# HGRN outputs summed from the last chunk, and weight splits and row-tile steps held behind the next operand at stage boundaries

## The chip, the cores and the metric

The kernel runs on one core of one Trainium2 chip. The metric is device time in microseconds (us) of one execution. Five engines work side by side, each through its own queue in order: TensorE (PE, matmuls; PEld is its weight load), VectorE (DVE), ScalarE (ACT), GpSimd (POOL) and SyncE (SP, which here issues all the DMAs). A matmul writes into one of 8 PSUM banks; everything else lies in SBUF.

## The reference, cut to what matters

A backbone of two layers over 512 latent tokens and 256 context tokens of width 1024. Each layer is a half-step SwiGLU, a token mixer and a half-step SwiGLU; each of these ends in a post-norm update. The mixer of layer 0 is a bidirectional HGRN (a gated linear recurrence in both directions, 8 heads), that of layer 1 a chunked spatial-gating MLP.

```python
def modulate(x, m, k):
    return x * (1 + m[..., 3 * k + 1, :]) + m[..., 3 * k, :]

def post_norm_update(x, y, m, k, g, b):
    return layer_norm(DN_ALPHA * x + m[..., 3 * k + 2, :] * y, g, b)

def macaron_half_ffn(x, m, k, w_in, w_out, g, b):
    return post_norm_update(x, 0.5 * swiglu(modulate(x, m, k), w_in, w_out), m, k, g, b)

# HGRN, per head: S_t = diag(f_t) S_{t-1} + k_t v_t^T,  o_t = S_t^T q_t, in chunks
o = (o_intra + o_inter)                 # inside a chunk + from the state before it
o = o_forward + reversed(o_backward)    # both directions
o = o * rsqrt(mean(o * o) + eps) * norm_w * silu(g)
```

For a token chunk s of a head the output is thus a sum of three products: the forward queries with the forward state before s, the backward queries with the backward state after s, and the scores inside the chunk with the values.

## The kernel before

**Precision.** Every big matmul is done in three: each operand is split into a high part (`fp32r`, rounded) and the rest. `split` (L134) makes the high part on ACT (L135) and the rest on DVE (L136). `mm3` (L146) multiplies high by high (L148), high by rest (L149) and rest by high (L150). `unit` (L139) loads one weight block of 128x1024 into a tile `raw` (a ring of 3) by an SP DMA (L141), takes a tile `w` (a ring of 6) and splits the one into the other.

**A stage's end.** `OutPhase.run` (L406) multiplies the hidden rows `h` by the output weights into four PSUM banks `y` (one for each 128-token tile), one half of the width (`hf`) after the other. Of the second half, the last `tail` pairs of blocks are not multiplied as they come: `held` (L426) loads and splits them first, and then goes tile by tile, so that the first token tiles are finished early. Then come, in the order in which the code is written:

- `operand_cols` (L430) and `nxt.load()` (L431): the next stage's first weights are loaded and split;
- `part` for each tile; where the next stage has `hold` set, the last two held blocks of the last tile are kept back as `rest` (L434);
- `done(0)` (L439): `evac` (L353) and `norm` (L364) of tiles 0 and 1: L357, L359 or L361, and L362 on DVE for each half tile, L367 and L369 on DVE, a power on POOL (L371), and L381 on DVE, which writes the normalised rows;
- the next operand: `operand` (L383), eight steps of two 128-column blocks for two token tiles. One step is four transposes on PE (L391), one scaling on DVE (L403) and one on ACT (L401), and a split (L135, L136). With `hold`, two of these steps come first, then `rest`, then `done(1)` (tiles 2 and 3), then the six other steps mixed with `nxt.staged`, the next stage's first matmuls, in the order that the string `order` gives (L508, L827).

The next stages: `FeedContext` (L779) and `HgrnValues` (L796) have `hold = False`; `FeedSums` (L741) and `GateIn` (L824) have it set. The `OutPhase` behind the HGRN has `tail=4` (L1306) and a `FeedSums` behind it; the two of the first SwiGLU have `tail=2` (L1045 for the latent tokens, with `FeedContext` next, and L1054 for the context, with `HgrnValues` next: its weights are `hg_wi`); the others with a next stage have `tail=3`. The very last has `tail=4` and no next stage. `FeedSums.rest` goes on with `seven` (L655), whose first call queues its DVE work behind the latest split.

**The HGRN.** The loop over heads (L1309) works on the projections of head h while head h-1 is finished. `latent_states` (L1252) goes through the four token chunks, forward for direction 0 and backward for direction 1; at each chunk it writes the scaled state `Sc` (L1262), which `outputs` (L1273) multiplies. So the forward states come in the order of chunks 0, 1, 2, 3, and the backward ones 3, 2, 1, 0. `outputs` sums the three products of each chunk into a bank `po` (L1280 forward, L1281 backward, L1282 inside the chunk) for s = 0 to 3, and normalises them (L1285 ACT, L1287 and L1288 DVE, L1290 POOL, L1292 DVE). `gated` (L1296), a head later, transposes the result (`pto`, L1298).

**What sets the order.** The code above is traced in program order; a scheduler then fixes each engine's queue, taking of the instructions that it holds to be ready the one traced first. On the chip the queues are fixed. `tc.issue_after(ins)` puts what is traced inside its block on the engine of `ins` behind `ins` in that engine's queue: it orders, and adds no wait for the end of `ins`. Other engines, the DMA queue among them, are not bound by it.

## Time and profile before

| | us |
|---|---|
| median of 3 runs | 2452.76 |
| lowest and highest of them | 2450.28, 2453.76 |
| the profiled execution, its own time | 2451.28 |
| its span, first to last instruction | 2449.6 |
| PE busy | 2415.6 (99%) |
| DVE busy | 1963.5 (80%) |
| ACT busy | 1151.4 (47%) |

The profiled execution's time lies 1.5 us below the median. Matmuls overlap in the records: one of 512 columns is shown with some 0.39 us, while in a full pipeline the next starts 0.227 us later, so a gap on PE is read from the starts. The view of waits shows what an engine was idle for, the chain of waits which work set the end, and the view by windows the busy time of each engine and the granted TensorE clock (PEclk) in one stretch.

The stretches that the change touches, by the span's clock: the end of the first SwiGLU for the latent tokens at 365 to 390 us, its end for the context at 550 to 585, the HGRN loop at 640 to 955, and the boundary behind it at 955 to 1030.

### The profile page before, as it was taken

To read this page: it belongs to the slowest core of one execution; us is meant where nothing else is said; L and a number is where in the kernel's file an instruction comes from. 1 tells how busy PE (TensorE), PEld (TensorE's weight loads), DVE (VectorE), ACT (ScalarE), POOL (GpSimd) and SP (SyncE) were. 2 spreads that over 40 slices of the span, in tenths; PEclk is the share of its full clock that TensorE was granted. 3 is DMA by queue.
4 is the path that set the end of the run, shared out by engine and by line. 5 is a ranking of instruction groups with operands and counts; after the bars stand their busy time and mean duration, and the time that the engine had idled before them with its cause. 6 is when DMAs were issued, how large, how long until landed. Compare 5 with 4: busy or idle time off the path is not lost.

```text
span 2449.6 us, 38155 instructions
## 1 busy us (share of the span) xinstructions
PE 2415.6 (99%) x14907; PEld 2185.6 (89%) x14907; DVE 1963.5 (80%) x3532; ACT 1151.4 (47%) x1784; POOL 34.0 (1%) x57
## 2 busy tenths in 40 slices
PE   7999999999999999999999999999999999999998
PEld 5888889987888888999988999988999988999987
DVE  7965679686488886988796988898898777988785
ACT  4222334454454452555643655544654443555641
POOL 0000000000000000000000000000000000000000
PEclk9999999999999999999999999999999999999999
DMA  8866465874211113433474333584323365333452
GB/s 324 299 204 202 164 196 191 285 243 149 70 54 57 61 52 112 152 111 104 139 237 154 108 104 104 156 261 140 122 84 96 116 219 173 132 118 104 138 162 79
DMA packets 107429, 366.01 MB, mean 149 GB/s; under 512 B 12472, under 2 KB 13808, under 8 KB 107248
## 3 DMA queue, kind: packets, MB, share of 16 engines
q1 hardware_dynamic: 107248, 363.58, 45.0%
q8 instruction: 116, 1.90, 0.3%
q14 instruction: 65, 0.53, 0.1%
HBM read 350.92 MB, written 12.61 MB: 148 GB/s over the span
## 4 chain that ended last, share of the span: by engine, by line
PE 83%; DVE 11%; ACT 3%; issue 2%; DMA 1%; POOL 0%; SPq 0%; DVEq 0%; POOLq 0%; ACTq 0%
PE y L150 9%; PE y L148 9%; PE y L149 9%; PE psf L150 6%; PE psf L149 6%; PE psf L148 5%; PE psc L148 5%; PE psc L149 5%; PE psc L150 5%; PE pse L150 3%; PE pse L148 3%; PE pse L149 3%; DVE w L136 1%; PE psa L150 1%; PE psa L149 1%
## 5 line engine op out<-in xcount | busy, mean ns | idle before, releaser
L136 DVE TENSOR_TENSOR w<-raw,w 128x1024 fp32r<-128x1024 f32 (+3 forms) x447 | 502.2, 1128 | 156.4 <-ACT w L135 152.3
L135 ACT ACTIVATE w<-raw 128x1024 fp32r<-128x1024 f32 (+3 forms) x447 | 436.4, 978 | 384.0 <-PE y L150 77.7
L150 PE MATMUL y<-w,hs 128*128 128x512 f32 x984 | 383.5, 390 | 1.2 <-DVE hs L136 1.1
L148 PE MATMUL y<-w,hs 128*128 128x512 f32 x984 | 383.9, 390 | 0.6 <-ACT hs L135 0.6
L149 PE MATMUL y<-w,hs 128*128 128x512 f32 x984 | 382.9, 389 | 0.0
L150 PEld LDWEIGHTS y<-w,hs 128*128 128x128 f32 x984 | 184.6, 188 | 42.0 <-DVE hs L136 3.8
L135 ACT ACTIVATE hs<-h 128x512 fp32r<-128x512 f32 (+1 forms) x220 | 126.4, 587 | 202.4 <-PE y L150 181.7
L148 PEld LDWEIGHTS y<-w,hs 128*128 128x128 f32 x984 | 184.7, 188 | 39.3 <-ACT hs L135 0.9
L149 PEld LDWEIGHTS y<-w,hs 128*128 128x128 f32 x984 | 184.8, 188 | 38.0
L148 PE MATMUL psf<-xm,w 128*128 128x512 f32 (+1 forms) x544 | 191.7, 356 | 14.3 <-ACT xm L1009 10.9
L150 PE MATMUL psf<-xm,w 128*128 128x512 f32 (+1 forms) x544 | 192.1, 354 | 1.2 <-DVE w L136 1.2
L149 PE MATMUL psf<-xm,w 128*128 128x512 f32 (+1 forms) x544 | 192.2, 354 | 0.1
L136 DVE TENSOR_TENSOR hs<-h,hs 128x512 fp32r<-128x512 f32 (+1 forms) x220 | 135.6, 637 | 65.7 <-ACT hs L135 65.5
L148 PE MATMUL psc<-f,w 128*128 128x256 f32 x544 | 154.3, 284 | 0.5 <-ACT sc L716 0.5
L150 PE MATMUL pse<-f,w 128*128 128x256 f32 x544 | 154.2, 284 | 0.1
L148 PE MATMUL pse<-f,w 128*128 128x256 f32 x544 | 154.0, 283 | 0.0
L150 PE MATMUL psc<-f,w 128*128 128x256 f32 x544 | 153.9, 283 | 0.0
L149 PE MATMUL psc<-f,w 128*128 128x256 f32 x544 | 153.9, 283 | 0.0
L149 PE MATMUL pse<-f,w 128*128 128x256 f32 x544 | 153.9, 283 | 0.0
L148 PE MATMUL psc<-xm,w 128*128 128x256 f32 x532 | 151.6, 285 | 0.6 <-ACT sc L716 0.6
L150 PE MATMUL psc<-xm,w 128*128 128x256 f32 x532 | 150.5, 283 | 0.0
L149 PE MATMUL psc<-xm,w 128*128 128x256 f32 x532 | 150.5, 283 | 0.0
(342 smaller groups left out, 6020.1 us busy)
## 6 DMA issues: line engine op xcount, KB each, us to landing
raw<-in_ffn_w_in SPq DMA_DIRECT2D x159, 512.0 KB, 4.6
raw<-in_ffn_w_out SPq DMA_DIRECT2D x110, 512.0 KB, 4.1
mraw<-in_mod_w SPq DMA_DIRECT2D x80, 512.0 KB, 4.6
rawu<-in_mod_w SPq DMA_DIRECT2D x64, 512.0 KB, 3.9
rawu<-in_ffn_w_in SPq DMA_DIRECT2D x60, 512.0 KB, 3.6
x<-x SPq DMA_DIRECT2D x36, 512.0 KB, 4.4
raw<-in_hg_wf SPq DMA_DIRECT2D x32, 512.0 KB, 3.5
raw<-in_cm_w_out SPq DMA_DIRECT2D x24, 512.0 KB, 4.7
```

Source lines behind the costliest of these rows:

```text
L135: nc.scalar.activation(dst_hi, src, AF.Copy)
L136: latest[0] = nc.vector.tensor_tensor(dst_lo, src, dst_hi.bitcast(F32), ALU.subtract)
L148: nc.tensor.matmul(ps, ah, bh, start=start, stop=False, **kw)
L149: nc.tensor.matmul(ps, ah, bl, start=False, stop=False, **kw)
L150: return nc.tensor.matmul(ps, al, bh, start=False, stop=stop, **kw)
```

## The change

1. In `outputs` the four chunks are summed in the order 3, 2, 1, 0.
2. Where the next stage is not on `hold` (the two ends of the first SwiGLU), all that `nxt.load()` traces on DVE is queued behind the latest split's DVE half, and all that it traces on ACT behind that split's ACT half. The latest split there is the last one of the held operands.
3. At the boundary behind the HGRN (`tail=4` and a next stage) only two of the four weight blocks are loaded at the old place. The DVE work of the first two operand steps and of `done(1)` (tiles 2 and 3) is queued behind the normalisation of tile 1, and the other two weight blocks are loaded after `done(1)`, their DVE halves queued behind the first operand step's split.

At the boundaries with `tail=3` the code does what it did.

```diff
     def split(dst_hi, dst_lo, src):
-        nc.scalar.activation(dst_hi, src, AF.Copy)
+        latest_hi[0] = nc.scalar.activation(dst_hi, src, AF.Copy)
         latest[0] = nc.vector.tensor_tensor(dst_lo, src, dst_hi.bitcast(F32), ALU.subtract)
...
-            nc.vector.tensor_scalar(z, z, mv[:, 0:1], rstd, ALU.subtract, ALU.mult)
+            self.normal = nc.vector.tensor_scalar(z, z, mv[:, 0:1], rstd, ALU.subtract, ALU.mult)
...
                 self.cols = operand_cols(self.l, self.j, *self.after, self.cond)
-                nxt.load()
+                if self.tail > 3:
+
+                    nxt.load(2)
+                elif nxt.hold:
+                    nxt.load()
+                else:
+                    with tc.issue_after(latest[0].ins), tc.issue_after(latest_hi[0].ins):
+                        nxt.load()
...
-                for i in range(2):
-                    self.operand(*steps[i])
-                for r in rest:
-                    self.part(*r)
-                close()
-                nxt.enter()
-                done(1)
+                with tc.issue_after(self.normal.ins) if self.tail > 3 else ExitStack():
+                    los = [self.operand(*steps[i]) for i in range(2)]
+                    for r in rest:
+                        self.part(*r)
+                    close()
+                    nxt.enter()
+                    done(1)
+                if self.tail > 3:
+                    with tc.issue_after(los[0].ins):
+                        nxt.load(2)
...
                 po = bank("po")
-                for s in range(NT):
+
+                for s in reversed(range(NT)):
                     o = po[:, s * P : (s + 1) * P]
```

## The prediction

> **What bounds the kernel now.** First the page: engine totals and the chain that ended last.

> ```profile
> PE 2415.6 (99%) x14907; PEld 2185.6 (89%) x14907; DVE 1963.5 (80%) x3532; ACT 1151.4 (47%) x1784; POOL 34.0 (1%) x57
> PE 83%; DVE 11%; ACT 3%; issue 2%; DMA 1%; POOL 0%; SPq 0%; DVEq 0%; POOLq 0%; ACTq 0%
> ```

> PE is the bound, and the change removes no matmul. It can only win places where PE stands still, so I next read PE's waits.

> ```profile
> ...
> PE pt L391 <- DVE x L381: 3.7, 4, 3.0
> PE po L1281 <- DVE Sc L1262: 2.5, 7, 0.4
> PE y L150 <- DVE hs L136: 1.1, 2, 0.6
> PE y L148 <- ACT hs L135: 0.6, 1, 0.6
> ```

> The row left out at the top is the kernel's start, which stays. These four are the change's three places. This view counts from a matmul's modelled end; below I use the starts, which show more.

> **Part 1, the context's end (L431, tail 2).** The chain of waits, then PE and ACT in order of time:

> ```profile
> 560.33 4.84 DMA raw<-in_hg_wi
> ...
> 565.19 1.07 ACT w L135
> ...
> 566.28 0.65 DVE w L136
> ...
> 567.42 0.43 DVE hs L136
> ```

> ```profile
> 565.49 0.50 PE L150 MATMUL y<-w,hs 128*128 128x512 f32 x1
> 566.60 0.50 PE L148 MATMUL y<-w,hs 128*128 128x512 f32 x1 [0.61 <-ACT hs L135]
> 566.94 0.39 PE L149 MATMUL y<-w,hs 128*128 128x512 f32 x1
> 567.90 0.50 PE L150 MATMUL y<-w,hs 128*128 128x512 f32 x1 [0.57 <-DVE hs L136]
> ...
> 571.47 0.39 PE L150 MATMUL y<-w,hs 128*128 128x512 f32 x1
> 571.70 0.39 PE L148 MATMUL psv<-w,xm 128*128 128x512 f32 x1
> ```

> The last operand's split waits on ACT and then on DVE behind the split of an `hg_wi` block that only the next stage needs. Full pace is 0.227 us (571.47 to 571.70). PE loses 566.60 - 565.49 - 0.227 = 0.88 and 567.90 - 566.94 - 0.227 = 0.73, together 1.61 us. The new edges put the four `hg_wi` splits behind that operand on both engines, so both losses go. What is late next: the four splits themselves. The blocks have three `raw` tiles, so the fourth block's DMA waits for the first block's split. That now ends about 567.4 (my estimate: the operand done near 565.3, when its own 0.8 on DVE no longer waits, then 1.07 on ACT and about 1.1 on DVE); with 4.84 for the DMA, 1.07 and 1.2 for its two halves it is ready at 574.5. `psv` would start at 571.70 - 1.61 = 570.1 and reach its fourth block after 18 matmuls, at 574.2. So 0.3 us may come back; bounds 0 (PE does the second tile's products first) and 1.61 (all comes back). I take a **gain of 1.4**. This stage's `evac` has three of these splits ahead of it, as traced first; its rows are not transposed before 582.58 (row in part 2), 10.9 after `y` ends: nothing.

> The same edit at 365 to 390 us holds two weight splits (1.2 us of DVE each) back until the last operand, just ahead of the evacuations. It costs nothing as long as this slack lasts:

> ```profile
> 379.07 0.81 DVE L381 TENSOR_SCALAR x<-x,mv,rstd 128x1024 f32<-128x1024 f32 x1
> 384.58 1.91 PE L391 MATMUL pt<-ident,x 128*128 128x128 f32 x16
> ```

> Tile 1's rows are done at 379.9 and transposed from 384.6: 4.7 us of cover, filled by the context's matmuls. Two splits in front would take 2.4 of it. With the cover gone it would cost up to 1.2.

> **Part 2, the boundary behind the HGRN.** The chain here (DVE's first row is a weight split, cut short by the chain's next step), and then the same stretch by windows (us; busy us of PE, PEld, DVE, ACT, POOL; PEclk; DMA):

> ```profile
> 979.81 0.28 DVE w L136
> ...
> 980.95 0.81 DVE x L381
> 981.76 1.13 DVE w L136
> 982.89 0.60 DVE st L362
> 983.50 0.59 DVE t L357
> 984.21 0.61 DVE x L359
> 984.88 0.66 DVE st L362
> 985.55 0.82 DVE x L381
> 986.42 1.55 PE pt L391 x6
> ...
> 1003.42 0.69 DVE xm L136
> ...
> 1027.53 0.39 PE pse L150
> ```

> ```profile
> 978.00:1003.40 25.40, 21.66 (x147) 19.43 (x147) 19.80 (x38) 11.76 (x19) 2.52 (x4) 0.93 0.40 145
> 1003.40:1027.50 24.10, 24.04 (x201) 23.83 (x199) 24.10 (x40) 15.29 (x25) 0.00 (x0) 1.00 0.40 141
> ```

> Transposes in order of time, here and at the context's end:

> ```profile
> 986.42 2.82 PE L391 MATMUL pt<-ident,x 128*128 128x128 f32 x12 [3.02 <-DVE x L381]
> 582.58 1.91 PE L391 MATMUL pt<-ident,x 128*128 128x128 f32 x16
> ```

> On the way to tile 1's rows (L381 at 985.55) DVE does two weight splits (1.13 each) and three steps of tile 2 (L357, L359, the second L362: 1.9). The edit takes all of these, some 4.2 us, out of the way: rows ready near 982.2 instead of 986.4. On PE's side the prize is larger. It waits 3.02, and after it the 12 transposes take 2.82 where 16 took 1.91: at a start every 0.11 that is 1.3 us too slow, and the windows show why, a PEclk of 0.93 over the stretch against 1.00. By PE's rows alone 4.3 us could go.

> But the work taken out is not gone: the 4.2 us of DVE move to between tile 1's rows and the last operand step, whose split is the row at 1003.42. From there the chain runs on DVE for 24 us without a hole (24.10 of 24.10 busy), since `seven` queues behind that split, and PE meets it at 1027.53. A faster PE before that only waits there. So the gain of this part is what the split at 1003.42 gains, and DVE has 25.40 - 19.80 = **5.6 us** idle before it. Part of the idle time is round trips (transpose, DVE, ACT, ACT, DVE), which stay. Bounds: a gain of 4.2, if all moved work falls into holes; a loss of 2.4, if the two late splits land in front of tile 3's rows and leave the holes behind. The rows lie in between; filling about half of the 4.2 gives a **gain of 2.1**.

> [...] The trace's slow transposes after 3.02 us of waiting agree with a clock halved there.

> Moved DMAs: the two late blocks' loads are bound by `raw` tiles as before (ready-first on SP), and the two `raw` tiles that they free come back late by as much as the splits move, for weights of the second and third hidden block, whose splits stand behind those at 1003.42 and after: hidden. The token rows' stores, which might now stand behind these loads on SP, are read back only by the next stage's end: nothing, unless they hold SP for 20 us.

> **Part 3, outputs from chunk 3.** In order of time: one head, its last backward state and PE around it; then the first use of head 6's outputs:

> ```profile
> 884.74 0.39 PE L148 MATMUL psfl<-xm,w 128*128 128x512 f32 x1
> ...
> 885.14 0.31 DVE L1262 TENSOR_SCALAR Sc<-S,se 128x128 f32<-128x128 f32 x1
> ...
> 885.50 0.49 PE L1281 MATMUL po<-Sc,B 128*128 128x128 f32 x2 [0.37 <-DVE Sc L1262]
> 885.83 0.39 PE L1282 MATMUL po<-v,ssum 128*128 128x128 f32 x2
> ```

> ```profile
> 928.50 0.39 PE L150 MATMUL y<-w,ht 128*128 128x512 f32 x1
> ...
> 929.15 0.66 PE L1298 MATMUL pto<-ident,on 128*128 128x128 f32 x4 [0.27 <-DVE on L1292]
> ```

> PE stands 885.50 - 884.74 - 0.227 = 0.53 us per head, seven times (the row of waits has 7): 3.7 us. The state waited for is that of chunk 0, the last of the backward direction. Chunk 3 first means that it is needed last, but it is still needed at the same place in DVE's queue, and the three chunks that now run earlier (2 us of PE) push out as much `psfl` filler. The filler stands in the queue up to where the scheduler held the state to be ready, in the middle of an `mm3` (L148, then L1281): PE will again arrive there 0.53 early, with the last chunk. I take **0** for the seven heads, bounds 3.7 (the wait goes) and -0.7 (a second break in each head: the pair at 885.50 takes 0.49 where the next pair takes 0.39, so a break costs 0.1 beside the wait). Three quarters of the sums are then done before the break, so the normalisation starts up to 2 us earlier, and the wait at 929.15 (0.65 - 0.227 = 0.42) goes: a **gain of 0.4**.

> **The sum.** 1.4 + 2.1 + 0.4 = 3.9 us off the profiled execution's 2451.28: 2447.4. That execution lies 1.5 below the median of 2452.76; off the median it is **2448.9**, my forecast, about 2449.

> **Rivals.**
> - *The heads' wait really goes.* For it: chunk 3's states are both there early, and only a quarter of the sums depends on the last one. Against: queues fixed by a schedule that is 0.53 off. Time: 3.7 more, 2445.2.
> - *All of the moved DVE work hides.* For it: 5.6 us of holes. Against: round trips. Gain 1.4 + 4.2 + 0.4 = 6.0: 2446.8.
> - *Nothing at the HGRN's boundary.* PE's wait moves from tile 1's rows to the two late weight splits, and operand 7's split comes no earlier: 2451.0.
> - *The clock halves again.* After tile 1's rows PE has transposes and short waits instead of matmuls; if that stretch counts as idle, 12 slow transposes cost 1.3 again: 2450.2. [...] In this trace 16 transposes at 582.58 ran at full pace, but behind matmuls.
> - *Slower.* The two late splits (2.4) come before tile 3's rows and the second half of the operand steps, whose holes stay: the row at 1003.42 comes 2.4 later, and the DVE chain behind it carries that to PE at 1027.53; with the clock's 1.3 on top the loss is 3.7, against gains of 1.8. It decides once those splits delay 1003.42 by more than 1.8. Time: 2452.76 + 1.9 = 2454.7.

> **Chances.** Forecast 0.40, heads 0.18, all hidden 0.13, nothing at the boundary 0.14, clock 0.06, slower 0.09. A measurement of this kernel can tell about 0.2% (4.9 us) from no change. Faster by more: the heads and all-hidden cases, and 0.12 of the forecast's (its own range is a gain of 2 to 6, 2446.8 to 2450.8): 0.43. Slower by more: 0.04, the slower case were it 3 us worse. Same: 0.53. The range reaches from 0.7 us of run-to-run room below the heads' case to just short of the slower one: 2444.5 to 2454.

> **What would show it.** In the changed kernel's profile: (1) no `hg_wi` split ahead of the context's last `hs` pair, and `y` matmuls 0.227 us apart up to `psv`. (2) L381 of tile 1 within 1 us of 982 on today's clock, no PE wait of 3 us before L391, PEclk 1.00; the last operand step's split some 2 us nearer to the HGRN's end, and still a DVE chain without a hole behind it. (3) L1281's wait still once per head, now at the last chunk; `pto` at the loop's end without a wait. It is wrong if the 0.53 before L1281 falls below 0.2, or if the split at 1003.42 moves by nothing or by 4 us.

## The result: slower, and only in the heads

| | us |
|---|---|
| before, median of 4 runs | 2453.26 |
| changed, median of 4 runs | 2482.91 |
| ratio, 95% interval | 1.0122 [1.0104, 1.0139] |
| span of the profiled execution, before and changed | 2449.6, 2481.5 |

The change costs 29.7 us. The page of the changed kernel, engine totals and the chain that ended last:

```profile
PE 2429.1 (98%) x14907; PEld 2199.3 (89%) x14907; DVE 1962.4 (79%) x3532; ACT 1150.8 (46%) x1784; POOL 34.1 (1%) x57
...
PE 86%; DVE 9%; ACT 3%; issue 1%; DMA 1%; POOL 0%; SPq 0%; DVEq 0%; POOLq 0%; ACTq 0%
```

PE has as many instructions as before and is 13.5 us longer busy with them: they ran slower. Then its waits (us in total, times, the longest):

```profile
PE po L1291 <- DVE Sc L1272: 25.9, 7, 3.7
...
PE pt L391 <- DVE x L381: 0.7, 3, 0.3
```

The lines have moved by ten or eleven: L1291, L1292 and L1293 are now the forward product, the backward one and the one inside the chunk (L1280 to L1282 before), and L1272 writes the scaled state (L1262 before). The wait of 3.0 us before L391 is gone, as forecast, and so are those of `y` for `hs`. The wait before `po` has grown from 0.4 to 3.7 us in each of seven heads (the eighth and last, whose queue holds other work there, waits in neither kernel), and it is another wait: L1291 is the *forward* product. One head, PE in order of time:

```profile
858.98 0.39 PE L150 MATMUL psq<-xm,w 128*128 128x512 f32 x1
863.07 0.80 PE L1291 MATMUL po<-Sc,B 128*128 128x128 f32 x2 [3.70 <-DVE Sc L1272]
863.66 0.63 PE L1292 MATMUL po<-Sc,B 128*128 128x128 f32 x2
...
866.65 0.63 PE L149 MATMUL psq<-xm,w 128*128 128x512 f32 x1
...
869.70 0.40 PE L150 MATMUL psq<-xm,w 128*128 128x512 f32 x1
```

and DVE in the same head:

```profile
860.05 0.28 DVE L1272 TENSOR_SCALAR Sc<-S,se 128x128 f32<-128x128 f32 x1
...
861.64 0.28 DVE L1272 TENSOR_SCALAR Sc<-S,se 128x128 f32<-128x128 f32 x1
...
862.75 0.67 DVE L1272 TENSOR_SCALAR Sc<-S,se 128x128 f32<-128x128 f32 x3
```

`psq` is the bank of two projections, q's and g's, each of 24 matmuls. The `psq` at 858.98 is the last of q's. All 24 matmuls of g's projection stand in the queue behind the first products of `po`. The first product is that of chunk 3 with its forward state, and this is the *last* state of the forward direction: the first of the three at 862.75, done at 863.03, 0.04 before PE starts. PE's queue holds nothing ahead of that product that PE could do until then. When it starts, an `mm3` matmul takes 0.63 instead of 0.39. The view by windows shows why; the rows are steps of 3.413 us, at whose ends the clock changes in this head (us; busy us of PE, PEld, DVE, ACT, POOL; PEclk; DMA share, GB/s):

```profile
854.64:858.05 3.41, 3.41 (x16) 2.82 (x15) 3.41 (x9) 0.06 (x1) 0.00 (x0) 1.00 0.32 130
858.05:861.46 3.41, 1.32 (x6) 0.75 (x4) 3.41 (x12) 2.05 (x5) 0.00 (x0) 1.00 0.00 0
861.46:864.88 3.41, 1.80 (x8) 1.80 (x9) 3.41 (x12) 2.42 (x5) 0.00 (x0) 0.50 0.00 0
864.88:868.29 3.41, 3.41 (x13) 3.00 (x12) 2.77 (x8) 0.00 (x0) 0.00 (x0) 0.50 0.52 154
868.29:871.70 3.41, 3.41 (x21) 2.97 (x20) 0.00 (x0) 0.43 (x1) 0.00 (x0) 1.00 0.00 0
```

After each wait the clock is at half for one or two such steps. All the seven stretches together, the first and the last of them and the sum:

```profile
690.80:697.62 6.83, 6.10 (x22) 5.52 (x23) 5.30 (x15) 1.54 (x3) 0.00 (x0) 0.50 0.28 77
...
946.80:953.62 6.83, 5.13 (x19) 4.75 (x20) 6.26 (x19) 2.50 (x5) 0.00 (x0) 0.50 0.25 77
sum 37.55, PE 31.27 PEld 29.42 DVE 34.00 ACT 11.97 POOL 0.00; mean PE 4.47 PEld 4.20 DVE 4.86 ACT 1.71 POOL 0.00
```

31.27 us of PE's work ran at a PEclk of 0.50; in the head above, matmuls of 512 columns then start 0.43 us apart (867.08 and 867.51) instead of 0.227. Taken as twice the time, from the 0.50 alone, that gives an estimate of 15.6 us for the clock. The waits grew by 25.9 - 2.5 = 23.4. Together 39.0 us for the seven heads; measured, by the stages below, are 37.6.

The stages, by the starts of three instructions: `psv`'s first matmul (the first product of `HgrnValues`), the last head's `pto`, and the first `psc` behind the HGRN (a bank of the SwiGLU that follows). Before:

```profile
954.72 0.28 PE L1298 MATMUL pto<-ident,on 128*128 128x128 f32 x1
...
1015.28 0.28 PE L148 MATMUL psc<-xm,w 128*128 128x256 f32 x1
```

and changed:

```profile
569.53 0.39 PE L148 MATMUL psv<-w,xm 128*128 128x512 f32 x1
...
990.13 0.27 PE L1309 MATMUL pto<-ident,on 128*128 128x128 f32 x1
...
1047.34 0.28 PE L148 MATMUL psc<-xm,w 128*128 128x256 f32 x1
```

`psv` starts 2.2 earlier (571.70 before); the heads take 420.6 instead of 383.0, 37.6 more; from the last `pto` to `psc` it takes 57.2 instead of 60.6, 3.4 less. By these two traces parts 1 and 2 gained what they were meant to and a little more; part 3 lost nearly seven times as much.

### The profile page after: what moved, and what is told of

Read it like the earlier page. It is cut to its first block, busy times and chain, and to the rows that moved or that the text cites. A ratio compares the mean times of both kernels' runs of the same rounds, so it can differ in the third digit from the quotient of the medians.

```text
span 2481.5 us, 38157 instructions
## 1 busy us (share of the span) xinstructions
PE 2429.1 (98%) x14907; PEld 2199.3 (89%) x14907; DVE 1962.4 (79%) x3532; ACT 1150.8 (46%) x1784; POOL 34.1 (1%) x57
## 4 chain that ended last, share of the span: by engine, by line
PE 86%; DVE 9%; ACT 3%; issue 1%; DMA 1%; POOL 0%; SPq 0%; DVEq 0%; POOLq 0%; ACTq 0%
PE y L150 9%; PE y L148 9%; PE y L149 9%; PE psf L150 5%; PE psf L148 5%; PE psf L149 5%; PE psc L148 5%; PE psc L150 5%; PE psc L149 5%; PE pse L150 2%; PE pse L148 2%; PE pse L149 2%; PE psa L150 1%; PE psa L149 1%; PE psa L148 1%
## 5 line engine op out<-in xcount | busy, mean ns | idle before, releaser
L136 DVE TENSOR_TENSOR w<-raw,w 128x1024 fp32r<-128x1024 f32 (+3 forms) x447 | 500.5, 1124 | 162.0 <-ACT w L135 161.2
L135 ACT ACTIVATE w<-raw 128x1024 fp32r<-128x1024 f32 (+3 forms) x447 | 436.0, 978 | 389.6 <-DMA raw<-in_ffn_w_in 80.3
L148 PE MATMUL y<-w,hs 128*128 128x512 f32 x984 | 383.7, 390 | 0.0
L150 PE MATMUL y<-w,hs 128*128 128x512 f32 x984 | 383.2, 390 | 0.0
L149 PE MATMUL y<-w,hs 128*128 128x512 f32 x984 | 382.9, 389 | 0.0
L135 ACT ACTIVATE hs<-h 128x512 fp32r<-128x512 f32 (+1 forms) x220 | 126.6, 588 | 211.1 <-PE y L150 192.7
L150 PEld LDWEIGHTS y<-w,hs 128*128 128x128 f32 x984 | 184.6, 188 | 39.7 <-DVE hs L136 1.3
L148 PEld LDWEIGHTS y<-w,hs 128*128 128x128 f32 x984 | 184.8, 188 | 38.4
L149 PEld LDWEIGHTS y<-w,hs 128*128 128x128 f32 x984 | 184.8, 188 | 37.8
L148 PE MATMUL psf<-xm,w 128*128 128x512 f32 (+1 forms) x544 | 191.5, 357 | 14.3 <-ACT xm L1019 10.8
L150 PE MATMUL psf<-xm,w 128*128 128x512 f32 (+1 forms) x544 | 192.6, 355 | 0.8 <-DVE w L136 0.7
L149 PE MATMUL psf<-xm,w 128*128 128x512 f32 (+1 forms) x544 | 192.3, 355 | 0.4 <-DVE xm L136 0.4
L136 DVE TENSOR_TENSOR hs<-h,hs 128x512 fp32r<-128x512 f32 (+1 forms) x220 | 135.2, 633 | 71.0 <-ACT hs L135 70.7
L148 PE MATMUL psc<-f,w 128*128 128x256 f32 x544 | 154.5, 284 | 0.7 <-ACT sc L726 0.7
L150 PE MATMUL pse<-f,w 128*128 128x256 f32 x544 | 154.3, 284 | 0.2 <-DVE w L136 0.2
L148 PE MATMUL pse<-f,w 128*128 128x256 f32 x544 | 154.0, 283 | 0.0
L150 PE MATMUL psc<-f,w 128*128 128x256 f32 x544 | 153.9, 283 | 0.0
L149 PE MATMUL psc<-f,w 128*128 128x256 f32 x544 | 153.9, 283 | 0.0
L149 PE MATMUL pse<-f,w 128*128 128x256 f32 x544 | 153.9, 283 | 0.0
L148 PE MATMUL psc<-xm,w 128*128 128x256 f32 x532 | 151.6, 285 | 0.6 <-ACT sc L726 0.6
L150 PE MATMUL psc<-xm,w 128*128 128x256 f32 x532 | 150.5, 283 | 0.0
L149 PE MATMUL psc<-xm,w 128*128 128x256 f32 x532 | 150.5, 283 | 0.0
```

The source lines that it names most:

```text
L135: latest_hi[0] = nc.scalar.activation(dst_hi, src, AF.Copy)
L136: latest[0] = nc.vector.tensor_tensor(dst_lo, src, dst_hi.bitcast(F32), ALU.subtract)
L148: nc.tensor.matmul(ps, ah, bh, start=start, stop=False, **kw)
L149: nc.tensor.matmul(ps, ah, bl, start=False, stop=False, **kw)
L150: return nc.tensor.matmul(ps, al, bh, start=False, stop=stop, **kw)
```

## The experiments

The same starts for every kernel that follows, in us; the first column runs from the last `pg` ahead of `psv` (a short matmul in the context's end, at 536.25 before) to `psv`, and each row is one profiled execution:

| kernel | `pg` to `psv` | heads | last `pto` to `psc` |
|---|---|---|---|
| before | 35.4 | 383.0 | 60.6 |
| changed | 33.4 | 420.6 | 57.2 |
| parts 1 and 2 alone | 34.6 | 382.9 | 57.4 |
| reversed order alone | 36.8 | 420.0 | 60.5 |
| bank opened | 33.3 | 384.2 | 57.3 |
| one step of g first | 33.2 | 384.0 | 57.7 |
| order 1, 2, 3, 0 | 33.5 | 387.1 | 57.4 |
| old order, in the next head | 32.9 | 378.9 | 57.1 |
| reversed, in the next head | 33.4 | 378.4 | 57.5 |
| 3 matmuls of g ahead | 33.4 | 414.9 | 57.2 |
| 6 matmuls of g ahead | 34.4 | 406.1 | 57.4 |
| 12 matmuls of g ahead | 32.9 | 387.0 | 57.5 |

### Which part costs

Parts 1 and 2 alone:

```diff
-                for s in reversed(range(NT)):
+                for s in range(NT):
                     o = po[:, s * P : (s + 1) * P]
```

> The changed kernel with the chunks summed in the old order 0, 1, 2, 3: parts 1 and 2 alone. Theory A (the reversed order alone made the loss; parts 1 and 2 gained 2.1 us up to psv and some 2.5 us behind the HGRN, by the starts in the two traces): 2453.3 - 4.6 = 2448.7, between 2447.5 and 2450; the seven waits before po are back at 0.4 each, 2.5 us in total, PEclk 1.00 through the head loop. Rival B (the edits of parts 1 and 2 changed the queues inside the head loop): waits of 3 us and a time above 2470 stay.

2446.74 us against 2451.54 for the kernel before, ratio 0.9978 [0.9969, 0.9988]. PE's wait before `po` is the old one, for the backward state (L1292):

```profile
PE po L1292 <- DVE Sc L1272: 2.4, 7, 0.4
```

The reversed order alone, in the kernel before:

```diff
-                for s in range(NT):
+                for s in reversed(range(NT)):
                     o = po[:, s * P : (s + 1) * P]
```

> The kernel before with the chunks summed in the order 3, 2, 1, 0 and nothing else. Theory A (the seven heads cost 37.6 us more by the starts of pto in the two traces, whatever the rest does): 2453.3 + 37.6 = 2490.9, between 2488 and 2493. Rival B (it costs this much only together with parts 1 and 2): under 2475.

2487.9 us, ratio 1.0145 [1.0132, 1.0158], with the same wait as in the changed kernel:

```profile
PE po L1280 <- DVE Sc L1262: 25.9, 7, 3.7
```

Both times lie just below their ranges (2447.5 to 2450, and 2488 to 2493). The kernel before ran at 2451.54 beside these, 1.7 under the 2453.3 from which the expectations were worked out, so the differences count: 4.8 gained where 4.6 was expected, 36.4 lost where 37.6 was. Theory A holds both times. Part 3 costs 36.4 us by itself, parts 1 and 2 gain 4.8. The parts add up: 36.4 - 4.8 = 31.6 against the 29.7 of the whole, within the intervals of some 0.2%.

### Why g's projection stood behind the products

All PSUM tiles of this kernel share one ring of eight banks. `outputs` is traced ahead of g's projection. Theory C: a bank is given to the tile traced later only once the earlier one has its own, and `po` takes its bank with its first instruction. In the old order that is the forward product of chunk 0, whose state is there early; the trace of before shows it as a single pair (one product is two matmuls) between q's last `psq` and g's first:

```profile
876.76 0.39 PE L150 MATMUL psq<-xm,w 128*128 128x512 f32 x1
876.99 0.38 PE L1280 MATMUL po<-Sc,B 128*128 128x128 f32 x2
877.13 0.48 PE L148 MATMUL psq<-xm,w 128*128 128x512 f32 x1
```

Reversed, the first instruction needs the last forward state, and g's matmuls would wait with it. The rival D is that the schedule merely took that state to be ready 3.7 us too early. Two edits tell them apart. The first gives `po` its bank early, by an instruction that needs nothing:

```diff
                 po = bank("po")
+                nc.tensor.transpose(po[:, 3 * P :], ident, ident)
```

> The changed kernel, order 3, 2, 1, 0, with one more 128x128 transpose of the identity into the bank po ahead of the products (overwritten by them). Theory C (the banks of one ring are given out in the order traced, so g's projection, traced behind po, can't be queued before po's first instruction, and that now needs the forward direction's last state): with the bank opened 14 of g's 24 matmuls (3.2 us) are queued ahead of the first product; its wait falls from 3.7 to about 0.5 to 0.7 per head, the clock stays at 1.00, and the time comes to that of parts 1 and 2 alone plus 7 x (0.1 for the transpose and 0 to 0.6 of wait): 2449.5 to 2453.5. Rival D (the schedule simply holds that state to be ready 3.7 us too early): a wait of over 3 us stays behind g's matmuls and the time is above 2470.

2447.24 us, ratio 0.9983 [0.9974, 0.9991]: below the expected 2449.5 to 2453.5, also by 0.2 when the range is counted from the 2446.74 of parts 1 and 2 alone. The transpose stands where the forward product of chunk 0 stood, 14 of g's matmuls follow, and then the products in the reversed order. PE in order of time and its waits:

```profile
837.78 0.27 PE L1288 MATMUL po<-ident 128*128 128x128 f32 x1
841.65 0.49 PE L1291 MATMUL po<-Sc,B 128*128 128x128 f32 x2 [0.38 <-DVE Sc L1272]
```

```profile
PE po L1291 <- DVE Sc L1272: 2.6, 7, 0.4
```

The second edit adds no instruction. The first of g's eight `mm3` is traced ahead of `outputs`; the bank tile is still asked for where it was:

```diff
-                    on = outputs(h - 1, prev)
-                    g, last = proj_silu(h - 1, 3, "g")
+                    ons, po = [], bank("po")
+                    g, last = proj_silu(h - 1, 3, "g", 1, lambda: ons.append(outputs(h - 1, prev, po)))
+                    on = ons[0]
...
         for k in range(KD):
             last = feat_k(ps, w, xm, k, c0, c1)
+            if k + 1 == at:
+                then()
```

> The changed kernel, order 3, 2, 1, 0, with only the tracing order turned: the first 3 of g's 24 matmuls are traced ahead of the outputs, and nothing is held. Theory C (g's projection is held back only because its bank is given out behind po's): g's bank is then given out first, 14 of its matmuls stand ahead of the first product, the wait of 3.7 us falls to 0.4 to 0.7 per head and the clock stays full: the time of the kernel with the opened bank less 7 x 0.1 for its transposes, 2446.5, between 2445 and 2449. Rival M (it was the added transpose that helped, by another way): waits of over 3 us and over 2470.

2447.68 us, ratio 0.9985 [0.9976, 0.9995]:

```profile
PE po L1292 <- DVE Sc L1274: 3.7, 7, 0.6
```

Rivals D and M fall: with the bank taken early the schedule itself puts 14 matmuls, 3.2 us, ahead of the first product, so it had the state's time to within 0.4 to 0.6 us. What it did not do, with the bank not yet taken, was put g's matmuls there. That the order in which banks are given out is the reason is what all three kernels of this part agree with; no run shows the inside of the scheduler. The expectation for the second kernel was 2446.5 and it came out 1.2 above, inside its range.

A third order tests theory C where nobody meant to help. Chunk 1 opens the bank:

```diff
-                for s in reversed(range(NT)):
+                for s in (1, 2, 3, 0):
```

> The changed kernel with the chunks summed in the order 1, 2, 3, 0. Theory C: the bank is opened by the forward state of chunk 1, which by the changed kernel's trace is there 1.1 us after q's projection ends (860.33 against 859.21): a wait of 1.1 for it, then 25 matmuls, and some 0.5 before the backward state of chunk 0: 7 x (1.6 - 0.4) over parts 1 and 2 alone, 2446.7 + 8.4 = 2455, the clock full (busy share of a window at least 0.68). Rival N (any order that does not begin with chunk 0 costs what the reversed one does): above 2475. Rival O (only the last forward state hurts): the time of parts 1 and 2 alone, 2446.7.

2449.98 us, ratio 0.9993 [0.9984, 1.0003]; PE in two heads:

```profile
841.61 0.49 PE L1291 MATMUL po<-Sc,B 128*128 128x128 f32 x2 [1.02 <-DVE Sc L1272]
849.64 0.39 PE L1292 MATMUL po<-Sc,B 128*128 128x128 f32 x2
...
879.70 0.49 PE L1291 MATMUL po<-Sc,B 128*128 128x128 f32 x2 [1.02 <-DVE Sc L1272]
```

The wait for the forward state of chunk 1 is 1.02, where the changed kernel's trace had given 1.1, and rivals N and O fall. The time alone tells C and O badly apart: 2449.98 lies 5.0 below the one's 2455 and 3.3 above the other's 2446.7. It is the seven waits of 1.02, 7.1 us in all, that decide. The 0.5 that I expected before chunk 0's backward state (the row at 849.64) did not come: PE comes to that product 9.4 us after q's last `psq` starts (840.20); in the kernel before it got there after 8.2 and then waited. That is 3.5 us of the 5.0; the other 1.5 stay open.

### Does the order cost anything by itself

Here the outputs of a head are traced inside the next head's first forget projection, so that they stand behind 15 of its 24 matmuls in the old order, or behind 12 in the reversed one. The seventh head has no such projection behind it; there they stand behind all of g's:

```diff
+                def late_outputs():
+                    if done:
+                        ons.append(outputs(h - 2, done[2]))
+
                 if h < NH:
-                    n0, last = proj_forget(h, 0)
+                    n0, last = proj_forget(h, 0, 5, late_outputs)
...
-                    on = outputs(h - 1, prev)
+                    if h == NH:
+                        ons.append(outputs(h - 1, prev))
```

The reversed kernel has 4 in the place of 5. `proj_forget` hands both to `feat_mm`, which calls `late_outputs` behind that step, as above.

> Parts 1 and 2, old order 0, 1, 2, 3, the outputs of a head traced inside the next head's first forget projection, behind 15 of its 24 matmuls (they stood behind 10). Theory E (the 0.53 per head is nothing but a queue place 0.53 us too early): the waits before po go, 3.7 us less than parts 1 and 2 alone: about 2445, and pto meets its rows without a wait. Rival F (the wait moves on, to pto or to the DVE chain): the same time as parts 1 and 2 alone, about 2448.7.

> Parts 1 and 2 and the order 3, 2, 1, 0, the outputs of a head traced inside the next head's first forget projection, behind 12 of its 24 matmuls. Theory K (only the place in PE's queue matters; the order of the chunks has no price of its own): no wait before po, the same time as the old order at that place, 2442.7, within 2441 to 2445. Rival L (the reversed order costs something by itself): over 2446.5, no better than parts 1 and 2 alone.

The old order gives 2442.65 us, ratio 0.9961 [0.9948, 0.9974], the reversed order 2441.38 us, ratio 0.9958 [0.9944, 0.9972]. PE in the old order's kernel:

```profile
842.60 0.39 PE L150 MATMUL psfl<-xm,w 128*128 128x512 f32 x1
842.83 0.38 PE L1293 MATMUL po<-Sc,B 128*128 128x128 f32 x2
```

0.23 us from start to start: no wait. So it is in six of the seven heads, in both kernels; the seventh keeps one wait, of 0.3 and 0.4. The heads take 4.0 us less than with parts 1 and 2 alone (378.9 against 382.9). Theories E and K hold in the main: the old wait was a queue place, and the order has no price to be seen once its place is right. E also expected `pto` to meet its rows without a wait; in the old order it still waits 0.28. Both versions beat both kernels, by 0.4% against the one before.

### Wait and clock apart

These kernels keep the reversed order, force 3, 6 or 12 of g's 24 matmuls ahead of the first product and queue the others behind it (`then` traces `outputs` and returns that first product; `at` is 1, 2 or 4):

```diff
-        for k in range(KD):
-            last = feat_k(ps, w, xm, k, c0, c1)
+        with ExitStack() as behind:
+            for k in range(KD):
+                last = feat_k(ps, w, xm, k, c0, c1)
+                if k + 1 == at:
+                    behind.enter_context(tc.issue_after(then().ins))
```

> The changed kernel, order 3, 2, 1, 0, with 3 of g's 24 matmuls put ahead of the first product and the other 21 held behind it: the wait of 3.7 us per head becomes 3.7 - 0.7 = 3.0. Theory G (the clock halves after a window of 3.413 us in which PE was busy for less than some 0.4 to 0.6 of it, wherever the pause lies): halved in most of the seven heads, and less time lost to it than in the changed kernel's 37.5 us at half clock. Theory H (it takes a pause of over 3 us, or a whole window without work): halved in few heads or none. Time by G about 2453.3 + 37 - 4.6 - 7 x 0.7 - some 3 = 2477.

> The same with 6 of g's 24 matmuls ahead: a wait of 3.7 - 1.4 = 2.3 us per head. Theory G: still halved in those heads whose pause falls mostly into one window (its busy share is then 1 - 2.3 / 3.4 = 0.32), not in those where two windows share it (0.66 each): between 1 and 6 of the seven heads, PEclk under 1.00 there. Theory H: in none; the time is then that of parts 1 and 2 alone plus 7 x (2.3 - 0.4) = 2446.7 + 13 = 2460. By G some 3 to 10 us more.

> The same with 12 of g's 24 matmuls ahead: a wait of 3.7 - 2.7 = 1.0 us per head, a busy share of at least 0.7 in every window. Theories G and H both: the clock stays full in all heads, and the time is 2446.7 + 7 x (1.0 - 0.4) = 2451.

| ahead of the first product | wait per head | heads followed by half clock | PEclk, 680 to 980 us | one run | kernel before |
|---|---|---|---|---|---|
| none (the changed kernel) | 3.7 | 7 | 0.94 | 2482.91 (median of 4) | 2453.26 |
| 3 | 3.0 | 7 | 0.95 | 2478.74 | 2451.29 |
| 6 | 2.3 to 2.4 | 6 | 0.97 | 2470.43 | 2451.29 |
| 12 | 1.0 | 0 | 1.00 | 2449.45 | 2451.29 |

The expected times were 2477, 2463 to 2470 and 2451, by theory G; the second came out 0.4 above its range. The kernel with 6 is the one that decides. Its first head and its second, in the clock's steps:

```profile
688.48:691.90 3.41, 1.95 (x9) 1.29 (x7) 3.41 (x13) 2.69 (x5) 0.00 (x0) 1.00 0.00 0
691.90:695.31 3.41, 2.60 (x19) 2.43 (x20) 3.41 (x11) 1.63 (x3) 0.00 (x0) 1.00 0.00 0
695.31:698.72 3.41, 3.41 (x22) 2.99 (x20) 1.98 (x6) 0.27 (x1) 0.00 (x0) 1.00 0.48 154
729.44:732.86 3.41, 1.04 (x8) 0.71 (x7) 3.41 (x14) 3.41 (x7) 0.00 (x0) 1.00 0.00 0
732.86:736.27 3.41, 3.41 (x15) 3.12 (x14) 3.41 (x8) 0.11 (x1) 0.00 (x0) 0.50 0.40 114
```

The pause is nearly the same in both: 2.28 and 2.37 us of wait. In the first head two steps share it (busy shares 1.95 / 3.41 = 0.57 and 2.60 / 3.41 = 0.76) and the clock stays full (PEclk 1.00); in the second it lies in one step (1.04 / 3.41 = 0.30) and the next step runs at half (0.50). In these runs theory G holds and H falls. In this kernel the heads lose 406.1 - 382.9 = 23.2 us: 16.4 - 2.4 = 14.0 by longer waits, and for six steps at half clock an estimate of 3.41 / 2 each, 10.2; the sum, 24.2, is 1.0 too much.

## Why the prediction was wrong

**Part 3 is the step that failed**: "I take **0** for the seven heads, bounds 3.7 (the wait goes) and -0.7". Measured: -37.6 in the two traces, -36.4 with the order alone. Two of its statements were false.

"chunk 3's states are both there early", in the first rival, holds for the backward one alone. The forward one is the last that the forward direction makes: the reversed products begin with it and stood 3.7 us in wait for it. I followed the backward direction alone, in which chunk 3 is the first.

"the three chunks that now run earlier (2 us of PE) push out as much `psfl` filler" took it that the reversed products would start where the old ones did and only change places with filler. The filler that was pushed out is not `psfl` at the back but all of g's projection at the front, because (as far as the runs above show it) `po`'s first instruction also opens its bank.

The bound -0.7 came from the price of a break, 0.1, as if the place of the wait were fixed. The trace of before held the rows for the true one: PE takes the first forward product up at 876.99 (shown above), and DVE writes the last forward state in the same head here:

```profile
880.51 0.69 DVE L1262 TENSOR_SCALAR Sc<-S,se 128x128 f32<-128x128 f32 x3
```

The first of these three is chunk 3's forward state. 880.51 + 0.28 - 876.99 = 3.8 us for a product that has to come at that place (by the starts, which give 3.8 to 3.9 for the waits of 3.7 in the changed kernel); seven times 26.6, and more where the clock falls behind such a wait, as it did at another place at the end of the 3.02 that the prediction had read (PEclk 0.50 from 985.83 to 989.24). The fall of the clock was named only as a rival of part 2, for 1.3 us. The slower rival named late weight splits, which cost nothing here.

"It is wrong if the 0.53 before L1281 falls below 0.2": at L1281's place (now L1292) it did fall to nothing, behind the larger wait.

The 0.4 at `pto` was right in size: in the changed kernel it follows its `y` matmul by 0.23 us (964.41 to 964.64). That the order does it is borne out by the two kernels with the outputs in the next head, 0.66 in the old order and 0.23 in the reversed one. With the bank opened, reversed too, it is 0.55: the gain depends on where the products stand.

**Part 1** was right in its mechanism and too small: 2.2 in this pair of traces against 1.4. The two losses of 0.88 and 0.73 are gone, the breaks of about 0.1 around them too, which the forecast had left out, and the 0.3 that "may come back" did not:

```profile
569.08 0.39 PE L149 MATMUL y<-w,hs 128*128 128x512 f32 x1
569.30 0.39 PE L150 MATMUL y<-w,hs 128*128 128x512 f32 x1
569.53 0.39 PE L148 MATMUL psv<-w,xm 128*128 128x512 f32 x1
```

By the table the stage took 32.9 to 34.6 us in ten kernels with the edit and 35.4 and 36.8 in two without, so one pair of traces gives this gain to about 1 us. No run has part 1 or part 2 without the other; they are told apart by these stages alone. At the first SwiGLU's latent end, where 0 was forecast, the first `psf` of the context starts at 378.76 against 378.83.

**Part 2** was right in its mechanism, and its size inside its bounds. The rows of tile 1, the last operand step's split, and the windows around the latter:

```profile
1017.10 0.81 DVE L381 TENSOR_SCALAR x<-x,mv,rstd 128x1024 f32<-128x1024 f32 x1 [0.68 <-POOL rstd L371]
```

```profile
1035.93 0.68 DVE xm L136
```

```profile
1013.41:1036.30 22.89, 21.32 (x153) 19.16 (x153) 19.91 (x39) 11.53 (x19) 3.06 (x4) 1.00 0.45 161
1036.30:1062.00 25.70, 25.47 (x210) 25.06 (x209) 25.63 (x41) 15.69 (x27) 0.00 (x0) 1.00 0.41 149
```

The HGRN ends 990.13 - 954.72 = 35.41 later here. Less that, L381 stands at 981.69 (forecast: within 1 us of 982), PE does not wait for it, PEclk is 1.00, and the split is at 1000.52 instead of 1003.42: a gain of 2.9 against the 2.1 forecast. DVE behind the split has no hole (25.63 busy of 25.70), as argued, though the chain view leaves it at 1050.39 for a weight load of 3.48 us, which it did not before PE took over at 1027.53. PE's own gain up to `psc`, 3.4, may then not all be kept: from there to the last matmul the two kernels without the edit took 1424.9 and 1425.7 us, the ten with it 1425.3 to 1426.4, on the mean 0.5 more, but the two ranges overlap. The rival in which the clock halves again did not come.

Parts 1 and 2 together were forecast at 3.5 us and measured 4.8 (ratio 0.9978 [0.9969, 0.9988]).

## What to carry to other kernels

Before a loop over results is turned round, write down for each result when its *last* input is ready in every direction, and ask what the first one does besides its sum: here, as far as the runs show it, it also takes the bank, and g's projection, traced behind it, stood behind its wait. Price a moved wait by the place to which it can move, not by the place at which it is now. To shorten a stall at the head of an in-order queue, move the instruction that waits behind enough filler (some 3.8 us here, by the rows above) before touching the order of the sums.

## What was not expected of the hardware

```profile
2439.90:2443.32 3.41, 1.49 (x7) 0.91 (x5) 3.13 (x5) 0.00 (x0) 0.00 (x0) 1.00 0.40 154
2443.32:2446.73 3.41, 0.00 (x0) 0.00 (x0) 3.27 (x7) 0.00 (x0) 0.92 (x1) 1.00 0.00 0
```

At half clock, the kernels' ends left out, steps with a share of 0.50 to 0.79 were followed by another at half (4) and steps with 0.83 or more by full clock (8). So the same wait of 3.7 us cost one step in three heads and two in the other four: where the wait reached far enough into the half-clock step (1.80 busy of 3.41 at 861.46, a share of 0.53), the next one was slow too. The 3.02 us before L391 in the kernel before, from which the prediction read a halved clock, are of the same kind, with work in the step before:

```profile
985.83:989.24 3.41, 2.82 (x12) 2.42 (x12) 2.95 (x7) 1.22 (x3) 0.49 (x1) 0.50 0.96 326
982.41:985.83 3.41, 0.99 (x6) 0.58 (x4) 3.40 (x8) 0.09 (x1) 0.56 (x1) 1.00 0.81 295
```

The share in which the state turns is read from records with modelled ends, so it is a share of the records.

No step had to be idle for it: 1.32 us of work in 3.41 (the step at 858.05) were followed by half clock. Pauses of 2.3 to 2.4 us were followed by it in six of seven heads, and of the four lengths tried (3.7, 3.0, 2.4 and 1.0 us) only 1.0 was not followed by it in any head.
